# Values behind the turns of queries and keys: the order of one head's steps in a hybrid attention and DeltaNet block

## The chip, the cores and the metric

The kernel runs on one core of a Trainium2 chip. A core has five engines that work side by side, each through a queue of its own in order: PE (matrix products and transposes), DVE (elementwise work), ACT (elementwise functions and copies), POOL (elementwise work) and SP, which here only issues DMA transfers. An instruction waits at the head of its queue until what it reads is written and what it overwrites is no longer needed; everything behind it on that queue waits with it. The metric is the time of one execution on the device in microseconds (us).

## The reference

One layer over 1024 latent tokens and 256 context tokens of width 1024. Half of the mixing width goes through neighbourhood attention, the other half through a gated DeltaNet with four heads. In the reference's words, cut to what matters here:

```python
h  = rmsnorm(x, g_pre) * (1.0 + scale) + shift          # hc: the same for the context
na_q, na_k, na_v, na_z, g_qkv, g_z, g_b, g_a = split(h @ w_in)
o_na = neighborhood_attention(na_q, na_k, na_v, na_kc, na_vc, rpb)
# gated DeltaNet: short convolution of 5 taps, silu, l2norm and rotation of q and k
q, k, v = silu(conv5(g_qkv))
q, k = rope(l2norm(q)), rope(l2norm(k))
# per chunk of 64 tokens, both directions: a triangular inverse ...
a     = strictly_lower(k*beta @ k.T * decay)
t_inv = solve(eye + a, eye)
# ... and then a scan over the chunks with a 128x128 state per head
y   = concat(o_na * silu(na_z), rmsnorm(o_g) * silu(g_z)) @ w_out
out = x + gate * rmsnorm(y, g_post)
```

All of it is float32 in and out.

## The kernel before, in words

The kernel is one program in stages, each written as Python generators that are advanced by hand; within that order a scheduler of the framework interleaves the instructions of neighbouring steps on each engine, so the order on a queue is near the written one and not equal to it. A product in float32 accuracy is made of three: the operands are split into a high part (`hh` of the modulated tokens, `wh` of a weight) and a low part (`hl`, `wl`), and `mm_chan` (line 157) issues hh x wh, hl x wh and hh x wl for each of eight slices of the width, so a projection of 512 latent tokens is 24 matmuls 128x512, one of the context 24 matmuls 128x256.

**Before phase 2** (phase 0) the tokens are normed, modulated and split. **Phase 2** goes over the four DeltaNet heads. For each head a string of letters is walked, one step to a letter:

- `Q`, `K`, `V`: `conv` (lines 877 to 902), the projection of queries, keys or values (tiles `gpc_*` for the context, `gpl_*` for the latent tokens) followed by the convolution: one scaled copy on ACT (L897), four taps on DVE (L899), tanh on ACT (L900) and a last DVE instruction (L901) that completes `acc_q`, `acc_k` or `acc_v`.
- `R`: `res_gate`, a part of the adaptive gates (L432 to L444).
- `p`: one step of `self.fill`, the generator `projections()` (line 865). It has 32 steps, each a projection that the head itself does not need: the gate paths (`pz`) and the attention's queries, keys (`pq`, `pk`) and values (`pv`). Here they are called filling steps.
- `T`: `qk_tok`, the turns of queries and keys from channels to tokens: PE transposes into `tp` (L921), ACT copies and squares (L924, L927), and for the keys a DVE product with the reciprocal norm into `tok` (L933); then the rotation (L943 to L945, on POOL for the queries and on DVE for the keys).
- `U`: the values' transposes into `vtp` (L838), a scaled copy on ACT and a transfer to DRAM.
- `B`: `qk_back`, which transposes `tok` back into `tb` (L956), copies it into `kq` on ACT and sends `kt` and `kq` to DRAM.

Ahead of the string stands `Q`, `K` and then `F` of the head before (`delta_front`, lines 1032 to 1067, which makes the triangular matrices out of `kq`). From head 2 on, after every letter one step of `blocks` is taken: the DVE's part of the triangular inverse, pairs of instructions at lines 1090 and 1093, for the group of an earlier head.

**Phase a2** (`phase_a2`, from line 1459) takes the filling steps that are left, some ahead of a loop, the others one per turn of the loop; in each turn it also advances by credits the last group of the triangular inverse and the merges (`inv_merge`, small matmuls 32 and 64 wide in tiles `tz` and `tu`, lines 1126 to 1186, with copies on DVE, ACT and POOL between them), which assemble the inverse of each head into `tm` and send it to DRAM (`tm_dram`).

**Phase b** interleaves the neighbourhood attention (`sc` scores at L763 and L766, POOL product `gm` at L754, DVE `nm` at L770, ACT `pt` at L771) with the scan (`pa` at L1272, L1283 and L1254). The scan's pool `g3` lies in SBUF where the pools of weights and of `hh` and `hl` lay, so its loads `tm`, `v`, `kt`, `kq`, `qe` can start only when the last filling matmul has read `hh`. A last phase multiplies with `w_out`.

The letters the change touches stand in phase 2 at line 856, the count ahead of the loop in `phase_a2` at line 1484.

Of the kernel before, what the change touches and what calls it, by code (L numbers as in the profile page):

```python
# [141 lines left out]
class K:  # L142
# [663 lines left out]
    def phase2(self):  # L806
        tc, nc, I = self.tc, self.nc, self.I
        ps = self.ps
        with tc.tile_pool(name="cv", bufs=1, side="right", reuse_waits="tile") as cv:
            self.yd = {}  # L810
            rope = cv.tile([P, 1536], F32, name="rope")
            nc.sync.dma_start(rope, I["rope"])
            self.ssq = self.cp.tile([P, 4, 8], F32, name="ssq")
            self.fill, self.ready = self.projections(cv), []
            kq, conv, toks = {}, {}, {}

            def step(h, c):
                if c in "QKV":
                    i = "QKV".index(c)
                    conv[c] = self.conv(cv, ps, 4 * i + h, f"{'qkv'[i]}{h}", i > 0)  # L820
                elif c == "p":
                    next(self.fill)
                elif c == "G":
                    self.gate_prep(cv, ps)
                elif c == "F":
                    self.delta_front(cv, ps, h, kq[h])
                elif c == "R":
                    self.res_gate(cv, ps, h)
                elif c == "T":
                    toks[h] = self.qk_tok(cv, ps, h, conv["Q"], conv["K"], rope)  # L830
                elif c == "B":
                    kq[h] = self.qk_back(cv, ps, h, toks[h])
                else:
                    for t0 in (0, 2, 6):
                        n = 2 if t0 == 0 else 4
                        pt = ps.tile([P, 4, P], F32, name=f"vtp{h}_{t0}", tag="tb", bufs=2)
                        for t in range(t0, t0 + n):
                            nc.tensor.transpose(pt[:, t - t0, :], conv["V"][:, self.col(t):self.col(t) + P], self.ident)  # L838
                        vs = self.wp.tile([P, 512], F32, name=f"vs{h}_{t0}", tag="st", bufs=4).rearrange("p (t c) -> p t c", t=4)
                        nc.scalar.activation(vs[:, :n, :], pt[:, :n, :], AF.Copy, scale=0.5)  # L840
                        nc.sync.dma_start(self.vt_dram[h][:, t0:t0 + n, :], vs[:, :n, :])

            blocks = iter(())
            for h in range(4):
                for c in "QK":
                    step(h, c)
                    next(blocks, None)  # L850
                for _ in blocks:
                    pass
                step(h - 1, "F") if h else step(h, "G")
                if h > 1:
                    blocks = self.inv_groups((h - 2,), lambda nm, n: cv.tile([P, n], F32, name=nm, tag=nm[:2]))
                for c in "RVppTppUB":
                    step(h, c)
                    next(blocks, None)
            step(3, "F")
            for _ in blocks:  # L860
                pass
# [590 lines left out]
    def phase_a2(self):  # L1452
        tc, ps = self.tc, self.ps
        with tc.tile_pool(name="a2", bufs=1, side="right", reuse_waits="tile") as ap:
            ready = self.ready
            buf = lambda nm, tag, n: self.pf.tile([P, n], F32, name=f"{nm}_{tag}", tag=tag)

            def blocks():
                vv = buf("ab", "vv", 2 * S)
                yield from self.inv_groups((2,), lambda nm, n: buf("tb2", "qh0", n) if n < S else vv[:, :S] if "ab" in nm  # L1460
                                           else vv[:, S:])
                self.mk = self.pf.tile([P, MTOT], mybir.dt.bfloat16, name="mk")
                self.load(self.mk, self.I["masks"])
                while len(ready) < 4:
                    yield
                self.na_pairs = {0: self.na_load(None, 0)}
                yield

            def merges():

                heads = [self.inv_merge(ap, ps, h) for h in range(4)]
                for c in MERGES.split():
                    h = int(c[0])
                    while c[1:] == "l" and (8 * h + 7) // 12 not in self.yd:
                        yield
                    next(heads[h])
                    if c[1:] == "e":
                        ready.append(h)
                    yield

            pr, gens = self.fill, (blocks(), merges())
            credit = [0.0, 0.0]
            first = True
            for _ in range(3):
                next(pr)
            for _ in pr:
                for i, (g, r) in enumerate(zip(gens, (3, 3))):
                    credit[i] += r
                    while credit[i] > 0:
                        if i:  # L1490
                            with tc.high_priority(offset=200):
                                next(g, None)
                        elif first:
                            first = False
                            with tc.high_priority(offset=300):
                                next(g, None)
                        else:
                            next(g, None)
                        credit[i] -= 1
            for g in gens:  # L1500
                for _ in g:
                    pass
# [66 lines left out]
```

## Time and profile before

| what | value |
|---|---|
| three runs | 872.26, 879.24 and 879.14 us, median 879.14 |
| profiled execution | 871.81 us, of which the profile's span is 870.1 |
| PE busy | 822.1 us, 94% of the span |
| DVE, ACT, POOL busy | 503.3, 418.4 and 355.7 us |
| mean granted clock of PE | 0.97 |
| DMA | 159.65 MB, mean 183 GB/s |

The profile is of one execution. "Busy" counts an engine's instructions, not how well it is used. The granted clock is the share of its full rate that PE was given in a stretch: 1.0 or about 0.5 in this trace. In a row of the timeline stand start, duration, engine, line, operation, result and operands, then in brackets the idle time just before it on its engine and what ended that. A row of a table by stretches (windows) has the stretch, its length, the busy time and count of PE, of PE's weight loads, of DVE, ACT and POOL, then the granted clock, the share of the DMA engines and GB/s.

### The profile page before, as it was taken

To read this page: it belongs to the slowest core of one execution; us is meant where nothing else is said; L and a number is where in the kernel's file an instruction comes from. 1 tells how busy PE (TensorE), PEld (TensorE's weight loads), DVE (VectorE), ACT (ScalarE), POOL (GpSimd) and SP (SyncE) were. 2 spreads that over 40 slices of the span, in tenths; PEclk is the share of its full clock that TensorE was granted. 3 is DMA by queue.
4 is the path that set the end of the run, shared out by engine and by line. 5 is a ranking of instruction groups with operands and counts; after the bars stand their busy time and mean duration, and the time that the engine had idled before them with its cause. 6 is when DMAs were issued, how large, how long until landed. Compare 5 with 4: busy or idle time off the path is not lost.

```text
span 870.1 us, 16462 instructions
## 1 busy us (share of the span) xinstructions
PE 822.1 (94%) x6082; PEld 698.2 (80%) x6082; DVE 503.3 (58%) x1051; ACT 418.4 (48%) x1087; POOL 355.7 (41%) x430
## 2 busy tenths in 40 slices
PE   6999999999999988988998998899999999999996
PEld 4788887888788776878886787788888988878885
DVE  3447165546635699869928953456666566653342
ACT  5356225744654653455315333466666666734210
POOL 2424031644362471228352100655657559624110
PEclk9999999999999998999999897699999999999998
DMA  9886442264454725652797489994967935134251
GB/s 334 315 286 224 133 134 88 83 202 160 123 187 150 210 85 164 201 136 67 239 257 236 155 202 309 415 226 127 303 177 260 252 96 180 41 110 133 86 185 68
DMA packets 86054, 159.65 MB, mean 183 GB/s; under 512 B 18373, under 2 KB 45334, under 8 KB 83798
## 3 DMA queue, kind: packets, MB, share of 16 engines
q1 hardware_dynamic: 78486, 144.94, 52.8%
q10 hardware_dynamic: 7488, 13.67, 5.1%
q8 instruction: 48, 0.79, 0.4%
q14 instruction: 32, 0.26, 0.1%
HBM read 109.51 MB, written 52.42 MB: 186 GB/s over the span
## 4 chain that ended last, share of the span: by engine, by line
PE 62%; DVE 16%; DMA 13%; ACT 3%; issue 3%; POOL 2%; SPq 1%; DVEq 0%; POOLq 0%; ACTq 0%
PE pz L157 5%; PE gpl_k L157 4%; PE gpl_q L157 4%; PE py L1381 3%; PE py L1382 3%; PE py L1383 3%; PE pk L157 3%; PE pv L157 3%; DVE vb L1093 3%; DVE tb L1090 3%; PE gpl_v L157 3%; PE pa L1272 3%; PE pq L157 2%; PE po L801 2%; PE pa L1283 2%
## 5 line engine op out<-in xcount | busy, mean ns | idle before, releaser
L771 ACT ACTIVATE pt<-pt,nm 128x544 f32<-128x544 f32 (+1 forms) x64 | 50.5, 790 | 38.2 <-DVE nm L770 37.9
L770 DVE CUSTOM_DVE_ANT_0 pt<-sc,gm 128x544 f32<-128x544 f32 (+1 forms) x64 | 49.4, 771 | 32.2 <-PE sc L766 26.5
L754 POOL TENSOR_TENSOR gm<-gt,mk 128x288 f32<-128x288 f32 (+1 forms) x48 | 46.6, 974 | 29.3 <-DVE nm L770 28.9
L1244 POOL TENSOR_SCALAR kd<-kt,kd 128x128 f32<-128x128 f32 x72 | 42.9, 609 | 21.2 <-PE pa L1283 21.1
L1032 ACT ACTIVATE em<-em,gc 128x128 f32<-128x128 f32 x80 | 25.6, 391 | 30.8 <-DMA em<-gc_dram 30.6
L157 PE MATMUL pz<-hh,wh_gz 128*128 128x512 f32 x96 | 38.2, 398 | 0.0
L157 PE MATMUL pv<-wh_nv,hh 128*128 128x264 f32 x128 | 36.7, 292 | 1.4 <-DVE st_z L568 0.8
L157 PE MATMUL pz<-hl,wh_gz 128*128 128x512 f32 x96 | 37.9, 395 | 0.0
L157 PE MATMUL pz<-hh,wl_gz 128*128 128x512 f32 x96 | 37.8, 393 | 0.0
L157 PE MATMUL pv<-wh_nv,hl 128*128 128x264 f32 x128 | 36.5, 288 | 1.1 <-DVE hl L273 1.1
L157 PE MATMUL pv<-wl_nv,hh 128*128 128x264 f32 x128 | 35.9, 286 | 1.4 <-DVE wl_nv L464 1.4
L1149 POOL COPY tm<-ld 32x320 f32<-32x320 f32 x16 | 7.3, 456 | 69.4 <-PE tz L1173 30.2
L899 DVE SCALAR_TENSOR_TENSOR acc_v<-xp_v,cols,acc_v 128x1282 f32<-128x1282 f32 x16 | 29.1, 1819 | 10.9 <-ACT acc_v L897 10.6
L1286 DVE SCALAR_TENSOR_TENSOR s<-s,egl,pa 128x128 f32<-128x128 f32 x64 | 19.6, 343 | 27.2 <-PE pa L1283 27.2
L1443 DVE TENSOR_TENSOR finv<-py,ggb 128x512 f32<-128x512 f32 x16 | 10.9, 689 | 41.7 <-ACT finv L1442 41.6
L1051 POOL TENSOR_SCALAR_AFFINE_SELECT qe<-qe 128x256 f32<-128x256 f32 x32 | 24.4, 765 | 25.0 <-DVE qe L1050 24.5
L1090 DVE TENSOR_TENSOR tb<-ab,vb 120x31 f32<-120x31 f32 (+15 forms) x62 | 29.1, 470 | 9.4 <-DMA ab<-ab_dram 7.8
L1250 POOL TENSOR_SCALAR vb<-v,beta 128x128 f32<-128x128 f32 x40 | 24.3, 608 | 20.9 <-DVE y L1256 17.8
L1442 ACT ACTIVATE finv<-py 128x512 f32<-128x512 f32 x16 | 9.5, 598 | 47.4 <-PE py L1383 29.3
L784 PE MATMUL tr<-c,pt 128*96 128x128 f32 (+1 forms) x192 | 32.0, 276 | 0.0
L782 ACT COPY tcx<-tc 128x256 f32<-128x256 f32 x64 | 23.5, 367 | 16.1 <-PE tc L780 15.7
L1047 DVE SCALAR_TENSOR_TENSOR pm<-pk,beta,em 128x128 f32<-128x128 f32 x80 | 23.6, 342 | 12.9 <-PE pk L1040 10.9
(432 smaller groups left out, 2857.6 us busy)
## 6 DMA issues: line engine op xcount, KB each, us to landing
wada<-in_w_ada SPq DMA_DIRECT2D x16, 512.0 KB
em<-gc_dram SPq DMA_DIRECT2D x20, 256.0 KB
pm_dram<-pm SPq DMA_DIRECT2D x20, 256.0 KB
tm_dram<-tm SPq DMA_DIRECT2D x8, 640.0 KB
kk<-qk_dram SPq DMA_DIRECT2D x16, 320.0 KB
tm<-tm_dram SPq DMA_DIRECT2D x4, 1280.0 KB
kq_dram<-kq SPq DMA_DIRECT2D x4, 1152.0 KB
kq<-kq_dram SPq DMA_DIRECT2D x4, 1152.0 KB
```

The lines of the kernel that those rows point to most:

```text
L157: r = self.nc.tensor.matmul(*a, **k)
L754: r = nc.gpsimd.tensor_tensor(self.gm[hh][:, 384 - n:384].rearrange("p (n c r) -> p n c r", c=nco, r=4), gv, self.mk[:, mo:mo + n].rearran ...
L770: nc.vector.tensor_tensor_reduce(pt[:, 384 - n:], sc[:, 512 - n:768], gm[:, 384 - n:], -1.0, 3.0e38, ALU.add, ALU.min, nm)
L771: self.last_exp = nc.scalar.activation(pt[:, 384 - n:], pt[:, 384 - n:], AF.Exp, bias=nm, scale=-1.0, accum_out=sums[:, ct, hh:hh + 1]).in ...
L784: self.pe(nc.tensor.transpose(pl[:m, rc * P:(rc + 1) * P], pt[:, 384 + (rc - 3) * m:384 + (rc - 2) * m], self.ident))
L899: nc.vector.scalar_tensor_tensor(av, xp[:, s0 + tap:s0 + tap + 1282 - s0], wc(tap), av, ALU.mult, ALU.add)
L1090: nc.vector.tensor_tensor(t3, bc(ab[:, 0:m, m:m + 1], [r, m, n]), bc(vb[:, m:m + 1, m:], [r, m, n]), ALU.mult)
L1093: nc.vector.tensor_tensor(vb[:, 0:m, m:], vb[:, 0:m, m:], t3, ALU.subtract)
L1244: r = nc.gpsimd.tensor_scalar(kd[d], kt_[:, t, :], self.kd[:, h, d, t:t + 1], None, ALU.mult)
L1272: self.pe(nc.tensor.matmul(pa, tm[:, d, t, :], y[d], start=True, stop=True))
L1381: nc.tensor.matmul(py, mh[:, tt], wh[:, nn], start=(k == W_ORDER[0]), stop=False)
L1382: nc.tensor.matmul(py, ml[:, tt], wh[:, nn], start=False, stop=False)
```

## The change

In each head the values' projection and convolution (`V`) move from ahead of the turns of queries and keys (`T`) to behind them; one filling step stands ahead of `T` and two behind `V`, where two stood between `V` and `T` and two behind `T`; the values' transposes (`U`) go behind the turns back (`B`). With three filling steps a head in place of four, four more are left for `phase_a2`: two more go ahead of its loop, and two more turns are made in it.

```diff
@@ phase2
                 step(h - 1, "F") if h else step(h, "G")
                 if h > 1:
                     blocks = self.inv_groups((h - 2,), lambda nm, n: cv.tile([P, n], F32, name=nm, tag=nm[:2]))
-                for c in "RVppTppUB":
+                for c in "RpTVppBU":
                     step(h, c)
                     next(blocks, None)
             step(3, "F")
@@ phase_a2
             pr, gens = self.fill, (blocks(), merges())
             credit = [0.0, 0.0]
             first = True
-            for _ in range(3):
+            for _ in range(5):
                 next(pr)
             for _ in pr:
```

What this does to the queues shows in three places.

On PE, in head 2, around the turns of queries (`tp_1_*`, of `acc_q`) and keys (`tp_0_*`, of `acc_k`), to the first turn back (`tb_0_0`); before:

```order
L157 MATMUL gpl_v_2825<-hh,wl_gv_4_2764 128x512
...
L157 MATMUL pk_0_2913<-hh,wl_nk_4_2872 128x512
L921 MATMUL tp_1_2_2950<-c_60,acc_q_2453 128x128 x4
L921 MATMUL tp_1_6_2965<-c_60,acc_q_2453 128x128 x4
L921 MATMUL tp_0_0_2989<-c_60,acc_k_2528 128x128 x2
...
L921 MATMUL tp_0_2_2997<-c_60,acc_k_2528 128x128 x4
...
L838 MATMUL vtp_0_3129<-c_60,acc_v_2769 128x128 x2
...
L956 MATMUL tb_0_0_3158<-c_60,tok_0_0_2992 128x128 x2
```

and now:

```order
L157 MATMUL gpl_v_2869<-hh,wh_gv_0_2827 128x512
L440 MATMUL pg_2673<-growg_2668,c_60 1x256
L921 MATMUL tp_1_2_2731<-c_60,acc_q_2379 128x128 x4
...
L921 MATMUL tp_1_6_2746<-c_60,acc_q_2379 128x128 x4
...
L921 MATMUL tp_0_0_2770<-c_60,acc_k_2454 128x128 x2
...
L921 MATMUL tp_0_2_2778<-c_60,acc_k_2454 128x128 x4
...
L157 MATMUL pq_1_2934<-hh,wh_nq_0_2683 128x512
...
L956 MATMUL tb_0_0_3021<-c_60,tok_0_0_2773 128x128 x2
```

The turns now lie inside the values' projection (`gpl_v`), where the projection and two filling steps (`pk_2`, `pk_0`) stood ahead of them; the values' turns (`vtp`) have left the stretch ahead of the turns back, and the filling steps `pq_1` and `pk_2` stand there.

On DVE, in head 2, the last instructions ahead of the keys' `tok` of L933; before:

```order
L901 SCALAR_TENSOR_TENSOR acc_v_2769<-xp_v_2768,acc_v_2769 128x1282
...
L1090 TENSOR_TENSOR tb_2755<-ab_2752,vb_2754 120x255
L568 SCALAR_TENSOR_TENSOR st_z_3119<-st_z_3119,pz_0_3094 128x512
L1093 TENSOR_TENSOR vb_2754<-vb_2754,tb_2755 120x17x15
L933 TENSOR_TENSOR tok_0_0_2992<-tp_0_0_2989,rq_y_g_3025 128x256
```

and now:

```order
L1090 TENSOR_TENSOR tb_2681<-ab_2678,vb_2680 120x240
L899 SCALAR_TENSOR_TENSOR acc_v_2839<-xp_v_2838,cols,acc_v_2839 128x1282
L1093 TENSOR_TENSOR vb_2680<-vb_2680,tb_2681 120x20x12
L899 SCALAR_TENSOR_TENSOR acc_v_2839<-xp_v_2838,cols,acc_v_2839 128x1282
L1090 TENSOR_TENSOR tb_2681<-ab_2678,vb_2680 120x247
L933 TENSOR_TENSOR tok_0_0_2773<-tp_0_0_2770,rq_y_g_2806 128x256
```

Behind the keys' L901 and ahead of `tok` stood all four taps of the values, their L901, three `sl_k` of filling steps and 30 instructions of the inverse; now two taps and 25 of the inverse stand there, and the rest comes behind `tok`.

On SP, at the end of `phase_a2`, the first loads of the scan; before:

```order
L1186 DMA tm_dram_87<-tm_4389 128x1280
L163 DMA tm_5742<-tm_dram_85 128x2560
L1186 DMA tm_dram_87<-tm_4391 128x1280
L163 DMA v_5740<-vt_dram_81 128x1280
L163 DMA kt_5741<-kt_dram_77 128x1280
L163 DMA kq_5739<-kq_dram_69 128x2304
L163 DMA qe_5743<-qe_dram_89 128x2048
```

and now:

```order
L1186 DMA tm_dram_88<-tm_4317 128x1280
L569 DMA z_dram<-st_z_5669 128x512
L163 DMA zs_0_5724<-z_dram 128x512
L163 DMA zs_1_5726<-z_dram 128x512
L569 DMA z_dram<-st_z_5698 128x512
L163 DMA tm_5742<-tm_dram_85 128x2560
L163 DMA v_5740<-vt_dram_81 128x1280
L163 DMA kt_5741<-kt_dram_77 128x1280
```

The loads stood ahead of the third head's second `tm_dram`; now all of the merges' transfers and the gate path's (`z_dram`) stand ahead of them. On PE the merges (`tz`, `tu`) of heads 2 and 3 stood alone behind the last filling matmul `pz_1`; now they lie between the filling steps, and `pz_1` is the last before the attention's `sc`.

## The prediction

> **What bounds the kernel now.** I read the page first, then PE's waits, then the stretches around the heads and the merges, and last the timeline where PE stands still. One row of the page, in 40 slices of 21.75 us, shows the clock that PE was granted, in tenths:
>
> ```profile
> PEclk9999999999999998999999897699999999999998
> ```
>
> The dips stand in slices 16, 23, 25, 26 and the last. PE holds 94% of the span, so a change that keeps PE's work the same can only move its stalls and its clock. Who makes PE wait in the part that the change touches:
>
> ```profile
> PE tb L956 <- DVE tok L933: 6.4, 2, 3.5
> PE tz L1173 <- DVE xo L1164: 5.0, 2, 3.8
> PE tp L921 <- ACT sq L927: 2.2, 2, 1.8
> PE tu L1179 <- DVE tm L1183: 2.1, 1, 2.1
> PE tz L1140 <- DVE ld L1128: 1.6, 1, 1.6
> PE pv L157 <- DVE wl_nv L464: 1.4, 1, 1.4
> ```
>
> (total us, times, longest). The keys' turns back wait for `tok`, the keys' turns for the squares, the merges for their own copies. The stretches, from the first keys' turns to the scan's first use of a state, and within them those at half clock:
>
> ```profile
> 130.00:329.60 199.60, 194.66 (x1013) 159.43 (x1011) 118.53 (x168) 110.44 (x290) 90.26 (x90) 1.00 0.45 142
> 329.60:336.50 6.90, 6.11 (x16) 4.88 (x17) 6.87 (x15) 0.96 (x2) 0.00 (x0) 0.51 0.69 220
> 336.50:462.00 125.50, 119.74 (x710) 103.66 (x708) 91.62 (x189) 49.35 (x122) 52.65 (x54) 1.00 0.61 180
> 462.00:527.00 65.00, 60.74 (x929) 49.87 (x930) 48.56 (x97) 26.09 (x57) 8.87 (x12) 0.92 0.69 206
> 527.00:551.10 24.10, 19.10 (x362) 17.95 (x361) 8.49 (x17) 8.92 (x21) 7.57 (x15) 0.58 0.97 332
> 551.10:558.30 7.20, 6.26 (x26) 5.56 (x26) 2.79 (x7) 3.26 (x9) 4.97 (x8) 0.50 1.01 417
> ...
> 466.10:469.60 3.50, 3.50 (x9) 2.73 (x10) 3.50 (x5) 3.42 (x8) 1.81 (x3) 0.51 0.87 310
> 490.00:496.90 6.90, 6.90 (x32) 6.04 (x32) 6.27 (x16) 3.95 (x9) 0.58 (x2) 0.51 0.78 290
> 531.00:551.10 20.10, 16.22 (x312) 15.28 (x311) 6.00 (x13) 5.04 (x13) 5.78 (x11) 0.50 1.01 349
> ```
>
> Stretch less busy time is PE's idle time: 4.9 + 0.8 + 5.8 = 11.5 us in phase 2, 4.3 + 5.0 = 9.3 in the projections and merges of a2, 0.9 at the attention's start, 21.7 in all. PE's busy time at half clock is 6.1 + 3.5 + 6.9 + 16.2 + 6.3 = 39.0 us. What half clock costs, and the stall of head 2, stand in the timeline:
>
> ```profile
> 276.43 0.39 PE L157 MATMUL gpl_k<-hh,wl_gk 128*128 128x512 f32 x1
> 295.51 1.50 DVE L901 SCALAR_TENSOR_TENSOR acc_k<-xp_k,acc_k 128x1282 f32<-128x1282 f32 x1 [3.37 <-ACT xp_k L900]
> 301.84 0.21 DVE L1090 TENSOR_TENSOR tb<-ab,vb 120x31 f32<-120x31 f32 x1 [3.41 <-DMA ab<-ab_dram]
> 303.01 1.55 DVE L899 SCALAR_TENSOR_TENSOR acc_v<-xp_v,cols,acc_v 128x1282 f32<-128x1282 f32 x1
> 306.61 2.59 DVE L899 SCALAR_TENSOR_TENSOR acc_v<-xp_v,cols,acc_v 128x1282 f32<-128x1282 f32 x1
> 313.02 1.27 ACT L900 ACTIVATE xp_v<-acc_v 128x1282 f32<-128x1282 f32 x1 [5.96 <-DVE acc_v L899]
> 315.00 0.66 PE L921 MATMUL tp<-c,acc_k 128*128 128x128 f32 x4 [1.79 <-ACT sq L927]
> 315.72 2.58 DVE L901 SCALAR_TENSOR_TENSOR acc_v<-xp_v,acc_v 128x1282 f32<-128x1282 f32 x1
> 322.28 0.39 PE L157 MATMUL gpl_q<-hh,wl_gq 128*128 128x512 f32 x1
> 322.51 0.40 PE L157 MATMUL gpl_q<-hh,wh_gq 128*128 128x512 f32 x1
> 323.56 0.69 DVE L541 TENSOR_TENSOR sl_k<-pk,sh_k 128x512 fp32r<-128x512 f32 x1
> 328.56 0.42 DVE L1090 TENSOR_TENSOR tb<-ab,vb 120x255 f32<-120x255 f32 x1
> 329.83 1.61 DVE L933 TENSOR_TENSOR tok<-tp,rq_y_g 128x256 f32<-128x256 f32 x3
> 330.39 0.66 PE L956 MATMUL tb<-c,tok 128*128 128x128 f32 x2 [3.55 <-DVE tok L933]
> 331.28 0.63 PE L157 MATMUL gpl_q<-hh,wl_gq 128*128 128x512 f32 x1
> 331.70 0.63 PE L157 MATMUL gpl_q<-hh,wh_gq 128*128 128x512 f32 x1
> ```
>
> Starts of 512-wide matmuls lie 0.23 us apart at full clock and 0.42 at half, so 45% of half-clock time is lost: 17.5 us of 39.0 at most. In the merges and at the attention's start part of the time is latency that does not scale, and I take 40% there: 2.7 in phase 2 (6.1 x 0.45), 4.7 in a2 beside the fillings (10.4 x 0.45), 6.5 at the lone merges (16.2 x 0.4), 2.5 at the attention's start (6.3 x 0.4), 16.4 in all. So 21.7 + 16.4 = 38 us can be won or moved. All times are those of this execution, 871.8 us; the median of the three runs is 7.3 us higher, their lowest within 0.5 of it.
>
> **Phase 2, turns earlier.** The keys' turns need `acc_k`. In head 2 it is ready at 297.0, 20.2 us after the last `gpl_k` at 276.8. Until `tp_0_0`, PE now has F, the context's and 34 latent matmuls of the values, and one filling step: 58 x 0.23 = 13.5, 24 x 0.12 = 2.9 (half as wide, half the time), F, gates and the queries' turns about 6, together 22 us. Heads 1 and 3 stand alike; head 0 lacks F, and its convolution the inverse beside it. So the turns should just not wait, with about 2 us in hand. This is the thinnest cover of the change.
>
> The 1.79 and its follower (2.2 in all) at `tp` go: ACT stood for 5.96 us at the values' tanh, ahead of the squares; now that tanh lies behind the keys' squares.
>
> The 3.55 at `tb` does not simply go. DVE was busy without a break from 301.84 to `tok` at 329.83. Of that, two of the values' taps (2 x 1.55 to 2.59, taken 4.1), their L901 (2.5), three `sl_k`, one `st_z` and one gate instruction (each at most 0.69, together 2.9) and five late instructions of the inverse (5 x 0.42 = 2.1) now stand behind `tok`: 11.6 us. `tok` starts near 318.2 and `tb` could run at 318.8. But PE also comes earlier. From 276.8 to `tb_0_0` it has 109 matmuls of 0.23 (25.4), 48 of 0.12 (5.8), F and turns 6.9: it arrives at 314.9 and stands 3.9 us. Then `tb_0_2` waits for the rotation, which has two more taps and a filling's `sl_q` between its parts: 1.5 more. Ends for the two: 1 and 9. In head 3, where `tok` came last too (the other 2.9 of the 6.4), 19 instructions of the inverse leave its front, so I take 1 (0 to 3). The `pv` wait of 1.4 stays, at 1.2. Sum of phase 2: 7.6 idle in place of 11.5, gain 3.9. The 3.9 at `tb` would draw half clock again, as 3.55 did and the 2.9 of head 3 did not; I keep half of its 2.7 us, gain 1.3.
>
> **Phase a2, merges between fillings.** PE's work is the same; four more filling steps lie here. The merges of heads 2 and 3, alone for 24.1 us before with 5.0 idle, now have 24 x 0.23 = 5.5 us of filling between most of their steps, against about 0.5 to 1 us for each copy they wait for. Those of heads 0 and 1 now follow each other with parts of a filling between them (in one place 9 matmuls of `pq_0` and 11 of `pq_1`), where whole ones stood. I put 1.7 on the first `tz`, 3.3 on the first `tu`, 3.5 on the rest: 8.5 idle, in place of 9.3 (4 to 13, the far end being the old waits of 9.3 plus the 3.8 of `xo` once more). Half clock: with wide matmuls between all merges I take 4 (1.5 to 9) in place of 4.7 + 6.5, gain 7.2.
>
> The Trainium skill, TensorE: Matmul & The Clock Gate, Part 1, says that the clock halves after an idle window of about 3.4 us. The trace bears this out at 330 only: at 466.1, 490.0 and 531.0 half clock came with stalls of 1.2 to 2.1 (`tz` and `tu` above) among small matmuls. By the rule the 4 would be nothing.
>
> **The attention's start.** New here: `tm`, `v`, `kt`, `kq`, `qe` can be issued only when the last filling matmul has read `hh`, and now that matmul is the last before `sc`. Before, the merges lay between:
>
> ```profile
> 526.62 0.39 PE L157 MATMUL pz<-hh,wl_gz 128*128 128x512 f32 x1
> ...
> 529.94 0.69 DVE L568 SCALAR_TENSOR_TENSOR st_z<-st_z,pz 128x512 f32<-128x512 f32 x1
> 535.10 0.42 SPq L163 DMA_DIRECT2D tm<-tm_dram  x1
> ...
> 556.73 0.63 PE L1272 MATMUL pa<-v,tm 128*128 128x128 f32 x2
> 560.87 0.71 PE L1254 MATMUL pa<-s,kq 128*128 128x128 f32 x4
> ```
>
> `pz` ended at 527.0 and the scan asked for `tm` and `v` at 556.7, 21.6 us after the issue: hidden. Now, from the end E of `pz_1`: two steps make `st_z` (ACT and DVE, about 0.7 each), then SP, on which the loads stand behind that `z_dram`, issues `tm` at E + 2. `tm` and `v` are 1.97 MB (128x2560 and 128x1280 in float32), at the 349 to 417 GB/s of the stretches above 4.7 to 5.6 us, and some latency: `v` lands at E + 8.5 (7.5 to 11). PE has scores, context products and a wait for the mask product (POOL, whose first `gm` must also wait for E) until about E + 5.5, so it stands 3 at `pa`, then about 1.3 at L1283 for `kd` out of `kt`, and 2.5 at L1254 for `kq` (`kt` and `kq`, 128x3584, are 1.84 MB more at that rate, 4.4 to 5.3 us). Behind SP's loads only the next pair's `kk` and `qh` wait, which are not needed yet. Idle 7 in place of 0.9 (4 to 12). The half clock of 551 to 558 cost 2.5; with such waits I leave 1.5 of it.
>
> **Sum.** Idle: 7.6 + 8.5 + 7 = 23.1 in place of 21.7, lost 1.4. Half clock: 1.4 + 4 + 1.5 = 6.9 in place of 16.4, won 9.5. Together 8.1 us faster: 864 against 871.8, or 871 against the median. The gain is the clock's; the stalls only change places.
>
> **The rivals.**
> - *No half clock without a stall above 3 us*: then a2 loses nothing to it and head 2's 3.9 alone draws it, as does perhaps `pa`. Half clock costs 2.7 and the sum is 16.4 - 2.7 - 1.4 = 12 faster: 860. For it: the 1.79 at 315.0 drew none, nor did the two waits of head 3. Against: the three stretches named. The rule of the Trainium skill's page on the clock gate, above, would bring this about.
> - *The load stall eats it.* If other transfers share the queues (DMA share 1.01 there) and `v` lands at E + 13, the start of the scan loses 5 more, and half clock lies over it for 2 more: 871, no change.
> - *Slower: the keys' turns wait for the keys' convolution.* Before, two filling steps and the whole values' projection covered `acc_k`; now 22 us against 20.2. It decides if L901 slips by more than 2 us a head, say because POOL's instructions slow the taps as at 306.61 (2.59 for 1.55; four taps give 4). A slip of 5 costs 3 in each of four heads, each with 2.7 of half clock if it reaches that far in half of them: 12 + 5 = 17, so 881, 9 slower. Against: ahead of `acc_k` nothing is added on DVE, and the values' work leaves.
>
> **How the numbers follow.** Chances: forecast 0.50, full clock 0.21, load stall 0.13, slower 0.16. What can be told from no change here is about 1%, 8.7 us. The forecast's own ends, from the terms (half their spread, since they do not all fall together), are 4 and 12 us faster: 860 to 868, or 867 to 875 on the median's scale. I state 867, between the two scales. The range goes from 855 (the full-clock case and some of the far ends) to 879 (the load stall on the median's scale), leaving out most of the slower case. Faster by over 1%: 0.21 and two fifths of the forecast, 0.41; within: 0.30 + 0.13 = 0.43; slower: 0.16.
>
> **What would show it.** Right: no wait of `tp` for `sq` L927; `tb` for `tok` still 3 to 5 us in head 2; no stretch of merges alone; the clock at 1.0 from the last filling into `sc`; a wait of `pa` L1272 for a load or for `vb`, 2 to 5 us; loads issued 2 us after the last `pz`. Wrong: a wait of `tp` for `acc_k` L901 in several heads; half clock for over 15 us in the a2 stretch; a `pa` that does not wait, since then 5 to 7 us more are won.

## The result and the profile after

The change makes the kernel slower by about half a per cent: median 880.31 us over 20 runs (873.82 to 886.31) against 874.16 over 20 runs of before (870.26 to 881.45), ratio 1.0058, 95% interval 1.0039 to 1.0078. The forecast was 8 us of gain. The profiled execution after took 875.2 us with a span of 873.4, 3.3 us longer than before's 870.1.

The page of after, engines and granted clock:

```profile
PE 818.2 (94%) x6082; PEld 689.3 (79%) x6082; DVE 493.3 (56%) x1051; ACT 417.1 (48%) x1087; POOL 352.4 (40%) x430
PEclk9999999999999989999989999899999999999999
```

PE has 3.9 us less of busy time than before for the same matmuls, so the clock did give something back; but the span grew by 3.3, so PE's idle time grew by 7.2. Who makes PE wait now (total us, times, longest):

```profile
PE tb L956 <- DVE tok L933: 8.7, 2, 5.3
PE tz L1140 <- issue: 6.9, 1, 6.9
PE pa L1272 <- DMA v<-vt_dram: 6.1, 1, 6.1
...
PE sc L763 <- DVE nm L770: 2.2, 2, 2.0
...
PE tb L956 <- DVE tok L945: 0.9, 1, 0.9
...
PE pg L440 <- ACT growg L434: 0.8, 1, 0.8
PE pk L1042 <- DVE qe L1050: 0.8, 1, 0.8
```

The many small waits of the merges are gone, as is the wait of the keys' turns for the squares. Three larger ones stand in their place. The first is that of the turns back, in head 2 and again in head 3 (the last row), as the timeline of after has it:

```profile
266.72 0.40 PE L157 MATMUL gpl_k<-hh,wl_gk 128*128 128x512 f32 x1
...
285.74 1.50 DVE L901 SCALAR_TENSOR_TENSOR acc_k<-xp_k,acc_k 128x1282 f32<-128x1282 f32 x1 [1.76 <-ACT xp_k L900]
...
293.39 0.45 DVE L1090 TENSOR_TENSOR tb<-ab,vb 120x31 f32<-120x31 f32 x1 [5.83 <-DMA ab<-ab_dram]
293.87 1.25 DVE L1093 TENSOR_TENSOR vb<-vb,tb 120x31 f32<-120x31 f32 x1
...
311.25 1.61 DVE L933 TENSOR_TENSOR tok<-tp,rq_y_g 128x256 f32<-128x256 f32 x3
...
311.71 0.69 PE L956 MATMUL tb<-c,tok 128*128 128x128 f32 x2 [5.27 <-DVE tok L933]
...
389.22 0.69 PE L956 MATMUL tb<-c,tok 128*128 128x128 f32 x2 [3.43 <-DVE tok L933]
```

DVE stands idle for 5.83 us until the inverse's matrices (`ab`) have come from DRAM, with the inverse's instructions at the head of its queue, then works through 25 of them and two of the values' taps, and only then comes to `tok`. The second large wait is that of the first merge, 6.86 us:

```profile
441.79 1.25 DVE L1126 STREAM_TRANSPOSE vx<-vl 128x1024 f32<-128x1024 f32 x1 [22.97 <-DMA v_dram<-vt]
...
444.36 0.84 DVE L1128 STREAM_TRANSPOSE ld<-vd 128x640 f32<-128x640 f32 x1
...
445.31 0.42 PE L1140 MATMUL tz<-ld,pmf 32*32 32x32 f32 x8 [6.86 <-issue]
```

The view has "issue" for it, which means that it found no releaser. `ld`, which the `tz` reads, ended at 445.2, 0.1 us before the `tz` started, so that is the likely one. In before the same pair is

```profile
463.73 0.83 DVE L1128 STREAM_TRANSPOSE ld<-vd 128x640 f32<-128x640 f32 x1
464.61 1.45 PE L1140 MATMUL tz<-ld,pmf 32*32 32x32 f32 x80 [1.61 <-DVE ld L1128]
```

So PE reached the merge 24.5 us earlier than in before (438.5 against 463.0), and `ld` was there only 19.4 us earlier (445.2 against 464.6). The third is at the attention's start:

```profile
546.57 0.39 PE L157 MATMUL pz<-hh,wl_gz 128*128 128x512 f32 x1
546.79 0.28 PE L763 MATMUL sc<-kk,qh 128*128 128x256 f32 x1
...
548.34 0.32 SPq L569 DMA_DIRECT2D z_dram<-st_z  x1
548.75 0.38 SPq L163 DMA_DIRECT2D tm<-tm_dram  x1
549.18 0.44 SPq L163 DMA_DIRECT2D v<-vt_dram  x1
...
558.07 0.77 PE L1272 MATMUL pa<-v,tm 128*128 128x128 f32 x2 [6.07 <-DMA v<-vt_dram]
...
564.22 0.71 PE L1254 MATMUL pa<-s,kq 128*128 128x128 f32 x4
```

The first `sc` follows the last `pz` at 546.8, `tm` goes out 2.0 us later as forecast, and `v` is there 8.9 us after its issue. The attention began 4.3 us sooner than in before (`sc` at 546.8 against 551.1), the scan's first L1254 came 3.35 us later (564.22 against 560.87), and that difference stays to the end: the stretch from there on is the same in both to 0.1 us.

The clock over the same parts, stretches of after:

```profile
310.10:316.90 6.80, 5.19 (x14) 4.14 (x15) 6.80 (x12) 0.37 (x1) 0.00 (x0) 0.50 0.23 80
388.60:392.00 3.40, 2.78 (x13) 2.78 (x14) 3.40 (x8) 0.91 (x2) 1.39 (x1) 0.50 0.38 111
443.20:450.00 6.80, 4.70 (x87) 4.28 (x88) 6.80 (x10) 5.51 (x12) 3.79 (x6) 0.50 0.51 171
555.80:562.60 6.80, 4.26 (x16) 3.61 (x17) 0.58 (x2) 1.48 (x4) 4.22 (x8) 0.50 1.06 423
```

PE's busy time at half clock fell from 39.0 us to 16.9, and each of the four stretches starts 2.8 to 4.8 us after the start of one of the large waits (306.4, 385.8, 438.5 and 552.0).

### The profile page after: what moved, and what is told of

It is laid out like the page before. It is cut to its first block, busy times and chain, and to the rows that moved or that the text cites. A ratio compares the mean times of both kernels' runs of the same rounds, so it can differ in the third digit from the quotient of the medians.

```text
span 873.4 us, 16440 instructions
## 1 busy us (share of the span) xinstructions
PE 818.2 (94%) x6082; PEld 689.3 (79%) x6082; DVE 493.3 (56%) x1051; ACT 417.1 (48%) x1087; POOL 352.4 (40%) x430
## 4 chain that ended last, share of the span: by engine, by line
PE 67%; DVE 13%; DMA 11%; ACT 4%; issue 3%; POOL 1%; SPq 1%; DVEq 0%; ACTq 0%; POOLq 0%
PE pz L157 7%; PE pv L157 5%; PE pk L157 4%; PE gpl_k L157 4%; PE py L1381 3%; PE py L1382 3%; PE py L1383 3%; PE gpl_q L157 3%; PE pa L1272 3%; PE gpl_v L157 3%; PE pa L1283 2%; PE po L801 2%; DVE tb L1090 2%; DVE vb L1093 2%; PE po L796 2%
## 5 line engine op out<-in xcount | busy, mean ns | idle before, releaser
L899 DVE SCALAR_TENSOR_TENSOR acc_v<-xp_v,cols,acc_v 128x1282 f32<-128x1282 f32 x16 | 27.2, 1700 | 24.1 <-ACT acc_v L897 23.9
L1051 POOL TENSOR_SCALAR_AFFINE_SELECT qe<-qe 128x256 f32<-128x256 f32 x32 | 21.0, 657 | 39.2 <-DVE qe L1050 39.1
L1090 DVE TENSOR_TENSOR tb<-ab,vb 120x31 f32<-120x31 f32 (+15 forms) x62 | 26.3, 424 | 13.8 <-DMA ab<-ab_dram 12.3
L787 ACT COPY tl<-tr 96x384 f32<-96x384 f32 (+1 forms) x64 | 30.5, 477 | 0.3 <-PE tr L784 0.3
```

The source lines that it names most:

```text
L787: nc.scalar.copy(tl[:m, :], pl[:m, :])
L899: nc.vector.scalar_tensor_tensor(av, xp[:, s0 + tap:s0 + tap + 1282 - s0], wc(tap), av, ALU.mult, ALU.add)
L1090: nc.vector.tensor_tensor(t3, bc(ab[:, 0:m, m:m + 1], [r, m, n]), bc(vb[:, m:m + 1, m:], [r, m, n]), ALU.mult)
```

## The experiments

There were two theories at first. TAIL: the loss is made at the attention's start, by loads that nothing hides any more. TURNS: it is made in phase 2, by turns back that wait for DVE. Each run's ratio is to before on the same chip. A ratio rests on 7 to 12 executions of the run, that of the count alone and that of the inverse behind `tok` in before on four. The code cuts are shortened.

**The order alone** (a1), with four filling steps a head as before:

```diff
-                for c in "RpTVppBU":
+                for c in "RpTVppBUp":
@@
-            for _ in range(5):
+            for _ in range(3):
```

> The order alone: the string is RpTVppBUp, so V stands behind T as in the change but a head has four filling steps as before, and three stand ahead of the loop in a2. Two theories of the 3.3 us that the changed kernel's profile is longer. TAIL: the loss is made at the attention's start, where the scan's loads now wait for the last filling matmul and nothing lies between it and the attention (from the last pz to the scan's first L1254 17.4 us where 9.8 were needed from sc on), while all ahead of it gained 4.3. TURNS: it is made in phase 2, where the turns back (tb) wait for tok as long as before or longer. Here a few merges (some 2 to 3 us) stand behind the last pz, and the cover between T and B is as in the change. TAIL: the wait of pa for v falls from 6.1 to about 3 and the time is 0.3% above before (0.999 to 1.005). TURNS: tb waits 8 to 9 us as in the change, and the time is 0.6% above before, the tail making no difference.

Measured: 1.0053 (1.0025 to 1.0081), as slow as the whole change. PE's waits in its profile:

```profile
PE pa L1272 <- DMA v<-vt_dram: 6.7, 1, 6.7
PE pz L157 <- DVE sl_k L541: 5.9, 1, 5.9
PE tb L956 <- DVE tok L933: 5.7, 1, 5.7
PE tp L921 <- DVE acc_k L901: 3.7, 1, 3.7
```

The ratio is near the 1.006 of TURNS, but its interval reaches well into TAIL's range (0.999 to 1.005), so the time does not decide. The waits show that neither theory has the whole of it: `tb` waits 5.7 us, not the 8 to 9 of TURNS; a `pz` waits 5.9 for DVE, which neither theory named; and the tail was not shortened. The merges behind the last `pz` hid nothing, since the last merge's `tm_dram` transfers stand ahead of the loads on SP and held them: `tm` went out 4.9 us after the last `pz` (556.1 against 551.2), in place of 2.0. And the wait that I had as the slower rival, the keys' turns for the keys' convolution, is there once, 3.7 us, in head 3.

**The count alone** (a2), three filling steps a head in the old order:

```diff
-                for c in "RpTVppBU":
+                for c in "RVppTpUB":
```

> The count alone: the string is RVppTpUB, the old order with three filling steps a head, five ahead of the loop in a2. Behind the last pz stand some 2 us of merges. TAIL: it costs what the late loads cost, less those 2 us, and the tb waits stay within 2 us of before (6.4): 0.4% above before. TURNS: with one filling step of 5.6 us less between T and B, tb waits 5 us more in heads 2 and 3 each: tb near 15 us and the time 1% or more above before.

Measured: 1.0130 (1.0062 to 1.0198), the slower end, where TURNS put it. The filling step missing between `T` and `B` shows at `tb` in one head (6.2, once) and at a values' filling:

```profile
PE tb L956 <- DVE tok L933: 6.2, 1, 6.2
PE pv L157 <- DVE st_z L568: 5.5, 1, 5.5
PE pa L1272 <- DMA v<-vt_dram: 5.2, 1, 5.2
```

but not with the 15 us that TURNS named. Neither part of the change is a gain by itself. With three filling steps the new order (1.0058, and 1.0076 in c1 below) looks better than the old one (1.0130), but these were measured on different chips, and the intervals overlap. The other edit of the change, five steps ahead of the loop of a2 in place of three, takes no part: with 3, 7 or 9 there, the changed kernel has the same instructions in the same order on PE, DVE, ACT and POOL, and on SP but for one load with 3. That was seen in the order, not timed.

**The loads cut in two** (a3). The scan begins with the two context tiles, but its first loads are whole heads:

```diff
@@ delta_load, first head only
-        for dst, src in ((tm, tm_dram), (v, vt_dram), (kt_, kt_dram), (kq, kq_dram), (qe, qe_dram)):
-            self.load(dst, src)
+        # tiles 0 and 1 of tm (both directions), v, kt and kq first, then the rest, then qe
+        for a, b, e in ((0, 2, 2), (2, 10, 18)):
+            self.load(tm[:, :, a:b], tm_dram[:, :, a:b])
+            self.load(v[:, a:b], vt_dram[:, a:b])
+            self.load(kt_[:, a:b], kt_dram[:, a:b])
+            self.load(kq[:, a:e], kq_dram[:, a:e])
+        self.load(qe, qe_dram)
```

> The changed kernel, with the loads of the scan's first head cut in two: the two context tiles of tm, v, kt and kq first (0.66 MB), the rest behind them. The order on all other engines is that of the changed kernel. TAIL: the first pieces land 4 to 5 us after the issue in place of 8.8, the wait at pa falls from 6.1 to 1.5 to 2.5 us, and the time is 4 us shorter: 1.001 of before (0.998 to 1.003). TURNS, or a rate limit: the wait only moves to L1283 or L1254, which need the later pieces, and the time stays at 1.005 or more.

Measured: 0.9974 (0.9944 to 1.0005), the gain that TAIL expected and a little more than its range, while TURNS had 1.005 or more. The wait at `pa` fell from 6.1 to under 1 us, but L1254 then waited 3.7 us for the later piece of `kq`, which is the give-back of TURNS in part.

**The inverse behind `tok`** (a4). The steps of the inverse are advanced after `V` and later, and the first instruction of a group is ordered behind the head's last `tok`:

```diff
-                for c in "RpTVppBU":
+                for i, c in enumerate("RpTVppBU"):
                     step(h, c)
-                    next(blocks, None)
+                    [next(blocks, None) for _ in range((0, 0, 0, 1, 2, 2, 2, 1)[i])]
@@ inv_blocks
+                m == 31 and self.order(d, self.last_tok)
```

> The changed kernel, with DVE's instructions of the inverse (L1090, L1093) of a head's group ordered behind that head's keys' tok (L933): nothing of the same group stands ahead of it any more, in head 2 nothing at all. TURNS: the tb waits (8.7 us, of them 5.3 in head 2) fall to 2 to 3 and the time by about 6 us, to 0.999 of before. TAIL: the tb waits fall alike, but the inverse ends later and the merges wait for it (the 6.9 us at the first tz grow by about as much), so the time stays within 2 us of the changed kernel's, 1.004 to 1.008.

Measured: 0.9966 (0.9937 to 0.9994). The 0.999 of TURNS lies in the interval, TAIL's range does not. In its profile, head 2:

```profile
305.38 1.62 DVE L933 TENSOR_TENSOR tok<-tp,rq_y_g 128x256 f32<-128x256 f32 x3 [1.89 <-POOL rq_y_g L177]
306.92 0.96 DVE L1090 TENSOR_TENSOR tb<-ab,vb 120x31 f32<-120x31 f32 x1
```

`tok` no longer waits behind the inverse but for its norm from POOL, and the two waits of `tb` for L933, 8.7 us, are one of 1.8. The first merge's wait did not grow, it fell to 1.7, so the gain ahead was not lost at the merges. The wait of `pa` for `v` is still 6.1. So both theories are right, each about a part.

**Both repairs together** (b1), on another chip, and with a third (b2), the context's keys as the last filling step:

```diff
@@ na_proj, last pair only
+                if i and p == 3:
+                    yield from self.gate_proj(ap, ps, p, 1536 + P * p)
-                for gr in (2, 0, 1)[1 - i:]:
+                for gr in (0, 1, 2)[:2 + i]:
```

> The changed kernel with both repairs: the inverse's instructions behind tok, and the scan's first loads cut in two. ADDITIVE (two separate costs, one in phase 2 and a2, one at the attention's start): each repair alone took 0.8 to 0.9% from the changed kernel, so 0.988 to 0.991 of before. SHARED (both only shift the same wait, since what is won ahead is waited for at the scan's loads): no more than one of them alone, 0.995 to 0.998.

> As the one before, and in the last of the filling projections the context's keys (24 matmuls 128x256, which do not read hh) come last, behind the gate path, so the scan's loads can be issued some 2.9 us before the last filling ends. ADDITIVE: another 1.5 to 2.9 us, 0.985 to 0.989. SHARED: no further gain, since with split loads the first pieces are no longer what is waited for.

Measured: 0.9980 (0.9960 to 1.0000) for both repairs, as SHARED expected, and 0.9952 (0.9927 to 0.9978) with the third, outside what ADDITIVE expected; the two intervals overlap, so that the third gains anything is likely and not shown. The third did not do what it was made for: its `v` was still waited for 2.5 us. The loads stood on SP behind the last merge's transfers:

```profile
540.62 0.93 SPq L1188 DMA_DIRECT2D tm_dram<-tm  x2
541.64 0.97 SPq L163 DMA_DIRECT2D tm<-tm_dram  x1
```

What made its gain, if it is one, was not followed.

**The same repairs on before** (b3 the inverse, b4 the loads).

> The kernel before the change (old string, four filling steps), with the inverse's instructions behind tok as in a4. If the waits of tb for tok (6.4 us in before) are a cost of the inverse's place and not of the change's order, this one gains too, 3 to 6 us at tb, and loses part of it at the merges, which then end later and stand alone longer: 0.995 to 1.003. If the gain of a4 belongs to the new order, nothing is won here, or it is slower: 1.000 to 1.008.

Measured: 1.0141 (1.0119 to 1.0163), worse than the range that a loss was given. In before's order the inverse comes so late that the merges wait:

```profile
PE tz L1140 <- DVE ld L1128: 16.2, 2, 9.2
PE tz L1173 <- POOL tm L1149: 7.5, 1, 7.5
```

The `tb` waits are gone here too. What they cost in before is less than what the later inverse costs.

> The kernel before the change with the scan's first loads cut in two as in a3. In before the loads are issued 21.6 us ahead of the scan, so by TAIL nothing is won: 0.998 to 1.002. If cutting the loads gains in itself (DMA traffic in better order), this one is faster by 0.5% too, and a3 did not show what it was taken to show.

Measured: 0.9970 (0.9952 to 0.9987). TAIL had expected nothing. So cutting the loads is worth 0.3% even where they were hidden, by something that I did not find, and not all of a3's gain can be put down to the wait at `pa`.

**Two by two on one chip**, since b1's chip had run neither the change nor one repair alone, and so left it open whether the repairs add up:

> The changed kernel itself, beside the three that follow on one chip, to set the two repairs against it directly. Over the runs so far the changed kernel's granted clock was 0.966 to 0.982 with spans from 872 to 884.5, and the profiled execution had the highest clock of all, so the profile shows a lucky one. Expected: 1.004 to 1.008 of before, a mean clock near 0.973 against 0.967 of before.

> The loads cut in two, alone, beside the others. Both theories: 0.996 to 1.000 of before. In the profile of a3 the scan's first L1254 came 7.3 us sooner than in the change, but the last phase's first py only 2.4: part of the win was given back at L1254, which waited 3.7 us for the later piece of kq.

> The inverse behind tok, alone, beside the others. Both theories: 0.995 to 0.999 of before, clock near 0.980.

> Both repairs together. ADDITIVE: their gains against c1 add up, within 2 us: with c2 and c3 at 0.998 and 0.997 and c1 at 1.006 it is 0.989. SHARED: it stays within 2 us of the better of c2 and c3, 0.995 to 0.999, as b1 did on another chip; then what one repair wins is lost where the other acts, and the comparison of the stretches says where.

| kernel | ratio to before | mean span | mean clock |
|---|---|---|---|
| before | 1 | 873.6 | 0.968 |
| the change (c1) | 1.0076 (1.0048 to 1.0103) | 879.7 | 0.971 |
| loads cut (c2) | 1.0023 (1.0004 to 1.0042) | 874.7 | 0.977 |
| inverse behind `tok` (c3) | 0.9984 (0.9961 to 1.0006) | 872.5 | 0.979 |
| both (c4) | 0.9935 (0.9911 to 0.9960) | 867.7 | 0.982 |

Against the change, the loads take 5.0 us of mean span, the inverse 7.2, both 12.0, each give or take 3: they add up, and c2 fell outside the range that I gave for it by 0.2%. The mean clock rises with each repair, so part of each gain goes with the clock: at the 0.51 us for 0.001 that is worked out below, an estimate, about 3 of the 5.0, 4 of the 7.2 and 5 to 6 of the 12.0. The profile of c2 still has both waits of `tb`, 8.7 us, and c3's still has the wait for `v`:

```profile
PE tb L956 <- DVE tok L933: 8.7, 2, 5.3
```

```profile
PE pa L1272 <- DMA v<-vt_dram: 6.2, 1, 6.2
PE tb L956 <- DVE tok L933: 1.6, 1, 1.6
```

(PE's waits, c2 first, c3 second.)

So two waits of the change are worth mending, each by itself, and with both mended the new order beats before by 0.65%. That the gain of the inverse's repair belongs to the new order is shown, since in before the same repair does harm (b3). For the loads it is open: cutting them took 5.0 us from the change but also 2.9 from before (b4, on another chip), where nothing waited for them, so as little as 2 of the 5.0 may be the cost of their lateness. For the same reason a fair rival of c4 would be before with its loads cut, which was 0.9970 on another chip; the two were not set side by side. Why both repairs together were 0.9980 on b1's chip and 0.9935 here stays open.

## Why the prediction was wrong, point by point

**The sum.** Forecast: idle time about even (1.4 lost), half clock 9.5 won, 8.1 faster. Measured between the two profiles: idle time 7.2 lost, PE's busy time 3.9 shorter, 3.3 slower. Both terms failed, the idle time by 5.8 us and the half clock by 5.6. Of the 5.8, phase 2 makes 3.6 (above all the turns back in head 3) and the attention's start 1.3; 1.1 lies outside the stretches of the forecast. The signs that I had named for being right nearly all came (no wait of `tp` for `sq`, a wait of `tb` in head 2, no merges alone, loads 2 us after the last `pz`), but none of them tested the price of half clock or head 3.

**Half clock, priced at 40 to 45%.** The price is 5.6 us of the error. The drop in half-clock time was forecast well for the profiled execution (39.0 to 16.9 us of busy time), and the price was wrong. The 45% came from 512-wide matmuls alone, and most of before's half-clock time lay over merges. Counting for each instruction the time by which it moves PE's end, from 60 to 560 us, the merges took 37.4 us in before, 17.1 of it at half clock, and 33.5 in after, 2.3 of it at half clock: 3.9 won, 26% of the 14.8 us that left half clock, where 7.2 stood in the sum for all of a2. Part of that is that the merges were slower in after even at full clock: L1181 took 49 ns each in before and 58 in after (108 at half clock in before); why was not followed. Over the runs of one kernel the price is as low: in 79 runs of before the span grows by 0.51 us for each 0.001 of mean clock lost, and in 27 of the change by 0.51. A clock lower by 0.001 is 1.75 us at half, so 0.51 is 29% of it.

**One profile for the clock.** The profiled execution of after had the highest clock of its 20 runs, 0.982, as one other had; their mean is 0.973, and that of 79 runs of before 0.968. In the mean run the change won 0.003 to 0.005 of clock; at 0.51 us for 0.001 that is 1.5 to 2.6 us, an estimate, and not 9.5. That the drop in half clock was forecast so well is in part the luck of this execution.

**Phase 2, idle 7.6 in place of 11.5.** Measured 11.2 (0.95 + 5.27 + 0.78 + 3.43 + 0.77): no gain. Head 2's turns back were right in sum, 5.27 for 3.9 + 1.5, and in their mechanism: `tok` behind the inverse, which a4 shows. That `tok` would start 21.2 us after `acc_k` failed a little: it was 24.0 (311.25 less 287.24), since DVE had to wait for `ab`, and six of the inverse's instructions took 1.2 to 1.5 us each in place of 0.2 to 0.4; these ran beside POOL's work (the end of the queries' rotation, L945, and the low parts of weights, L464). Head 3's 1 us was wrong: 3.43. I had counted the instructions of the inverse that left its front, and not asked how much earlier PE would come: 24.4 us (385.8 against 410.2), where `tok` came 23.7 earlier. There, other than in head 2, all four taps of the values, their L901 and 20 instructions of the inverse still stood ahead of `tok` in after. The wait of `pv` for its weights, which I kept at 1.2, went.

**The cover of the keys' turns.** In the change it held: no `tp` waits for `acc_k`, and the keys' turns start 0.8 to 5.0 us after it in the four heads (2.7 in head 2, where about 2 were forecast). The slower rival did not happen, but a1, which differs by one filling step, shows it in one head.

**Phase a2, 8.5 idle.** Right in sum, 8.3 (6.86 + 0.87 + 0.58), and wrong in kind. The merges between fillings hardly wait, and most of it is one wait at the first of them, for blocks that come from phase 2 by way of DRAM. It is a part of phase 2's gain in progress that was given back. It is 4.2 to 6.9 in the profiles of the change and of the cut loads (after, a3, c1, c2) and 0.8 to 3.9 in those with the inverse behind `tok` (a4, c3, c4).

**The attention's start, 7 idle.** The mechanism was right to the issue time, and the size a little low: 8.3 idle (1.99 + 6.07 + 0.27). `v` landed 11.3 us after the last `pz`, not 8.5; L1254 did not wait. From the last `pz` to L1254 it took 17.4 us. What the cut loads won is no clean measure of this wait, since they won in before too.

**The rivals.** The one that I had at 0.13, the load stall that eats the gain, is nearest to what happened, with the turns back beside it. The one at 0.21, no half clock without a long stall, describes after's profile: each of its four stretches begins within a wait of 3.4 us or more, and none lies over the 100 us of merges between fillings. That agrees with the Trainium skill, TensorE: Matmul & The Clock Gate, Part 1, on an idle window of about 3.4 us, in three of the four; the stretch at 388.6 began when PE had stood for 2.8 us, as did the one at 329.6 in before. In c1, the same program, a stretch at 512.6 had no wait ahead of it, and five other profiles of the new order (a4, b1, b2, c2, c3) have such stretches among the merges. So the rule does not hold in every execution, and that after's profile has none there is luck. The gain that I hung on it did not come, for the price above.

## What to carry to other kernels

Price a clock change from the instructions it falls on and from many runs, not from the widest matmuls of one profile. When work is moved ahead on one engine, ask of every engine and queue behind it whether it can come ahead too: here PE came early, and DVE's queue (an inverse waiting for DRAM ahead of a short instruction that PE needed) and the loads behind the last filling did not come as far. A change that looks lost can be worth keeping when its new waits have names, since two small repairs made this one 0.65% faster than before on one chip; but try each repair on the old kernel too, or its gain may be counted for the change.

## What the runs showed of the hardware

Executions of one program differ here by about 1.4% (873.8 to 886.3 us in 20 runs of the change), and the mean granted clock goes with it, 0.966 to 0.982, correlation -0.71 over 27 runs (with c1's). Half clock came in pieces of 3.4 us or twice that (6.8, 3.4, 6.8 and 6.8 us in after). In the traces of all 14 profiles the granted clock changes only at points of a grid of 3.41 us, and the grid lies elsewhere in each execution. So it is not the length of a wait alone that counts, but how it falls on the grid. Of 47 steps of the grid at full clock in which PE was busy for less than 44% (from 60 to 845 us), 46 were followed by half clock; of 3000 in which it was busy for more than half, 18 were, and in all 18 stood merges. Why merges draw half clock in some steps and not in others stays open. A load of 640 KB queued behind 1280 KB took 8.9 us from issue to its first reader, while the stretch from the last `pz` to L1254 (17.4 us) moved 312 GB/s on average.
